# A gate load moved from SP's DMA queue to ScalarE's, ahead of its scores, with four buffers

## The chip, the cores and the metric

The kernel runs on 1 core of one Trainium2 chip. The metric is the device time of one execution in microseconds, as the median over several runs. The core has five engines that take their instructions in order and wait for each other by semaphores: TensorE (PE), VectorE (DVE), ScalarE (ACT), GpSimd (POOL) and SyncE (SP). SP does no arithmetic here: it issues the DMAs, the transfers between HBM and the core's own memory, and each of them lands some time after its issue.

## The reference

The model has two layers over 2048 tokens of width 1024 and a context of 256. Layer 0 mixes with differential attention and a short convolution, layer 1 with a neighbourhood attention and a Fourier mix. The change lies in layer 1's neighbourhood attention, of which this is the core, for one row of the 32 x 64 token grid:

```python
def one_row(args):
    q_r, r0, roff = args
    kb = lax.dynamic_slice_in_dim(kg, r0, kh, axis=1)
    ...
    s_w = s_w + jnp.transpose(bias, (0, 2, 1, 3))[None]
    s_c = jnp.einsum('bqhd,bkhd->bhqk', q_r, k_c) * scale
    p = jax.nn.softmax(jnp.concatenate([s_w, s_c], axis=-1), axis=-1)
    ...
out_x = jnp.concatenate([o_n * jax.nn.silu(gn), fourier_mix(ud) * jax.nn.silu(gd)], axis=-1)
```

There are 8 heads of width 64. `silu(gn)` is the gate: a 512 x 2048 array that layer 1's input projection has written to HBM, and with which the attention's output is multiplied element by element.

## The kernel before

Layer 1's attention (`attention1`) works on 4 head pairs `hp`, and in each on 16 blocks `i` of 128 tokens, so on 64 blocks n = 16 hp + i. A block has two halves `hh`, one for each head. For each half `scores` computes six products on PE into PSUM (L1922), VectorE adds the bias or mask and takes the maximum (L1929), ScalarE takes the Exp with its sum (L1931), VectorE the reciprocal of the sum (L1933), GpSimd scales the row (L1934). `transposes` runs two blocks later: PE transposes the row in two pieces into tiles `pt` of a pool with two buffers (L1956), ScalarE copies the first piece to `pT`, VectorE the second (L1959, L1961). `values` runs three blocks later: PE multiplies `pT` with v into `po` (L1976). Four blocks share one `po`; below they are called a group, j = 0 to 15. At a group's last block VectorE multiplies `po` with the group's gate, in place of the gate (L1982), and SP stores the product to `mixa` in HBM (L1983). The gate g, 128 x 512 numbers or 256 KB, is loaded by SP at the group's first `values` (L1969), into two buffers; a buffer can be loaded again when the store out of it has landed.

While a pair is worked on, the next pair's data are loaded, in `scores` at the pair's first block: `na_q` (four halves of q at L1830, 512 KB each), `na_k` (eight of k at L1844, 576 KB each), `na_rest` (v at L1870, 1152 KB; the masks bm at L1880 and L1881) and the bias rows be of the edge blocks (`na_edge`, L1862, 128 KB each). All these are issued by SP too.

The code calls the steps in the order of the blocks, but the order of each engine's instructions is set by a scheduler with a model of durations (`schedule_with_timeline_sim`). Only what goes through `pin` keeps its order on its engine: here PE's products and transposes. DMAs aren't pinned in this stage. A DMA carries one of eight semaphores in turn (DMAHW0 to DMAHW7), whichever engine issues it, and waits for the DMA eight places before it in the scheduled order.

The stage begins while the Fourier mix ends: its last products Y are multiplied with another gate (`g<-gd`, L1784, L1786) and stored (L1787). It ends with the load of the output projection's weights (ws, L1241), which then runs on PE until 3309 us.

Of the kernel before, what the change touches and what calls it, by code (L numbers as in the profile page):

```python
# [9 lines left out]
F32 = mybir.dt.float32  # L10
# [7 lines left out]
P = 128  # L18
# [136 lines left out]
class Backbone:  # L155
# [45 lines left out]
    def pin(self, i):  # L201

        e = i.ins.engine
        if e in self.pinned:
            self.tc.add_manual_dep(i.ins, self.pinned[e].name, mybir.DependencyInfo(
                mybir.DependencyClass.NoSync, mybir.DependencyReason.DATA), reason="order")
        self.pinned[e] = i.ins
# [1676 lines left out]
    def attention1(self, qa, ka, rs, ws, ps_t):  # L1884

        nc, a = self.nc, self.a
        NK = self.NK
        with ExitStack() as es:
            qb = self.pool(es, "nqb", 1, "left")
            kb = self.pool(es, "nkb", 1, "left")  # L1890
            vp = self.pool(es, "nv", 2, "left")
            mp = self.pool(es, "nm", 2, "left")
            sp = self.pool(es, "ns", 4, "left")
            ep = self.pool(es, "ne", 2, "left")
            ps_s = [self.pool(es, f"nps{h}", 1, space=PSUM) for h in range(2)]
            ps_o = self.pool(es, "npo", 2, space=PSUM)
            self.pinned = {}
            pin = self.pin

            class It:  # L1900
                pass

            its = {}
            anchors = []

            def scores(n, hh):
                if hh == 0:
                    its[n] = It()
                it = its[n]
                hp, i = n // 16, n % 16  # L1910
                it.hp, it.i = hp, i
                st = self.na[hp]
                edge = i in self.EDGES
                nk = 512 if edge else NK
                kt0 = min(max(i - 2, 0), 12)
                if hh == 0:
                    it.s = []
                ps = ps_s[hh].tile([P, 1024], F32, tag="ps", name="ps")
                c0 = 768 - nk
                for p0, p1, kk in ((c0, 512, kt0 * P), (512, 768, kt0 * P + 512 - c0), (768, 1024, S)):  # L1920
                    for part in range(2):
                        pin(nc.tensor.matmul(ps[:, p0:p1], st["q"][hh][:, i * P:i * P + P],  # L1922
                                             st["k"][hh][part][:, kk:kk + p1 - p0], start=part == 0, stop=part == 1))
                w = nk + L
                s = sp.tile([P, NK + L], F32, tag="s", name="s", bufs=6)
                bias = (st["e"][i] if edge else st["m"])[hh]

                mx = ep.tile([P, 1], F32, tag="mx", name="mx", bufs=4)
                nc.vector.tensor_tensor_reduce(s[:, :w], ps[:, c0:1024], bias, -1.0, BIGGEST, ALU.add, ALU.min, mx)  # L1929
                Z = ep.tile([P, 1], F32, tag="Z", name="Z", bufs=6)  # L1930
                nc.scalar.activation(s[:, :w], s[:, :w], AF.Exp, bias=mx, scale=-1.0, accum_out=Z)  # L1931
                rz = ep.tile([P, 1], F32, tag="rz", name="rz", bufs=4)
                anchors[:] = [nc.vector.reciprocal(rz, Z).ins,  # L1933
                              nc.gpsimd.tensor_scalar(s[:, :w], s[:, :w], rz, 1.0, ALU.mult, ALU.mult).ins]  # L1934
                it.s.append(s)

                it.blocks = [(b * P, P, kt0 + b) for b in range(4)] + [(nk, P, 16), (nk + P, P, 17)]
                if not edge:
                    it.blocks.append((512, 64, kt0 + 4))
                if hh == 0:  # L1940
                    it.pT = [None, None]
                    return
                if i == 1 or i == 2:
                    self.na_edge(hp, 13 + i)
                if i == 0 and hp < 3:
                    self.na_q(hp + 1, qb if hp % 2 == 0 else qa)
                    self.na_k(hp + 1, kb if hp % 2 == 0 else ka)
                    self.na_rest(hp + 1, vp, mp)

            def transposes(n, hh):  # L1950
                it = its[n]
                pT = it.pT[hh] = sp.tile([P, 7, P], F32, tag="pT", name="pT")
                for g in (0, 4):
                    pt = ps_t.tile([P, 512], F32, tag="pt", name="pt")
                    for x, (o, m, kt) in enumerate(it.blocks[g:g + 4]):
                        pin(nc.tensor.transpose(pt[0:m, x * P:x * P + P], it.s[hh][:, o:o + m], self.ident))  # L1956
                    full = 4 if g == 0 else 2
                    srcp = pt.rearrange("p (k q) -> p k q", q=P)
                    (nc.scalar.copy if g == 0 else nc.vector.tensor_copy)(pT[:, g:g + full], srcp[:, 0:full])  # L1959
                    if len(it.blocks) > g + full and g:  # L1960
                        nc.vector.tensor_copy(pT[0:64, 6], srcp[0:64, 2])  # L1961

            def values(n):
                it = its[n]
                hp, i = it.hp, it.i
                if i % 4 == 0:
                    it.po = ps_o.tile([P, 512], F32, tag="po", name="po")
                    it.g = ep.tile([P, 512], F32, tag="g", name="g", bufs=2)
                    nc.sync.dma_start(it.g, self.gn[hp * P:hp * P + P, i * P:i * P + 512])  # L1969
                else:  # L1970
                    it.po, it.g = its[n - 1].po, its[n - 1].g
                oc = it.po[:, (i % 4) * P:(i % 4) * P + P]
                nb = len(it.blocks)
                for x, (o, m, kt) in enumerate(it.blocks):
                    for hh in range(2):
                        pin(nc.tensor.matmul(oc[64 * hh:64 * hh + 64], self.na[hp]["v"][0:m, kt, 64 * hh:64 * hh + 64],  # L1976
                                             it.pT[hh][0:m, x, :], start=x == 0, stop=x == nb - 1,
                                             tile_position=(0, 64 * hh)))
                if i % 4 < 3:
                    return  # L1980
                g = it.g
                nc.vector.tensor_tensor(g, it.po, g, ALU.mult)  # L1982
                nc.sync.dma_start(self.mixa[1][i // 4][hp * P:hp * P + P], g)  # L1983
                for k in range(n - 3, n):
                    its.pop(k)

            self.na_rest(0, vp, mp)
            fs, steps = ExitStack(), []
            for n in range(67):
                for hh in range(2):  # L1990
                    if n > 52 and steps:
                        self.pinned.update({i.engine: i for i in anchors})
                        steps.pop(0)()
                        if not steps:
                            fs.close()
                    if n < 64:
                        scores(n, hh)
                    if 2 <= n < 66:
                        transposes(n - 2, hh)
                if n >= 3:  # L2000
                    values(n - 3)
                if n == 49:

                    rs.close()
                    steps = self.load_wout(1, ws, fs)[1]
# [53 lines left out]
```

## Time and profile before

| what | value |
|---|---|
| median of 3 runs | 3306.8 us (3304.11 to 3309.04) |
| the profiled execution's own time | 3310.85 us |
| its span | 3309.1 us |
| PE busy | 3144.4 us, 95% of the span |
| DVE, ACT, POOL busy | 1922.6, 1581.1, 1450.1 us |
| DMA | 442.08 MB, mean 134 GB/s |
| layer 1's attention in the span | about 2757 to 3121 us |

The profile is of one execution, which took 4.05 us more than the median; times in the trace are counted from the span's start. A busy share over the whole span says little about a change in one stage. What has to be read is that stage's own stretch, the waits in it, and the order of SP's issues. In a row of a timeline stand the start and the length in us, the engine, the line, the operation, what it writes and reads, and in brackets the idle time before it and what ended it.

### The profile page before, as it was taken

The numbers are of one execution on the slowest core, as the hardware profiler recorded it, in microseconds if no ns is written. First come the engines' busy times: TensorE is split into PE (matmuls) and PEld (weight loads), VectorE is DVE, ScalarE is ACT, GpSimd is POOL, SyncE is SP. The second block draws the span as 40 slices with busy tenths as digits, with TensorE's granted clock in tenths as the row PEclk, the third lists the DMA queues.
The fourth block names the chain that finished last, engine by engine and source line by source line (L and its number), as shares of the span: only waits on it lengthen the run. The fifth ranks groups of instructions, "written<-read, shape, count | busy, mean of one in ns | idle before, by whom it ended". The sixth has DMA issues, their size and how long they took to land. (4 is left out here: it accounts for less than half of the span.)

```text
span 3309.1 us, 53756 instructions
## 1 busy us (share of the span) xinstructions
PE 3144.4 (95%) x20154; PEld 2618.1 (79%) x20154; DVE 1922.6 (58%) x4315; ACT 1581.1 (48%) x2541; POOL 1450.1 (44%) x1205
## 2 busy tenths in 40 slices
PE   7999999999999999989999799999999998899999
PEld 6988878777788778777877578898888887788787
DVE  4466564588888888888888745321121026566643
ACT  4311143577777778777777543421111124566410
POOL 3234200478887778777877743200121002343300
PEclk9999999999999999999999899999999999999999
DMA  7366653523343343323322144533232248963233
GB/s 259 119 213 224 218 147 115 190 99 107 125 129 109 100 151 100 128 91 112 119 98 69 59 156 153 176 110 125 74 108 98 84 151 228 225 147 105 69 136 121
DMA packets 305318, 442.08 MB, mean 134 GB/s; under 512 B 54837, under 2 KB 212001, under 8 KB 292258
## 3 DMA queue, kind: packets, MB, share of 16 engines
q1 hardware_dynamic: 305058, 438.64, 41.3%
q8 instruction: 160, 2.62, 0.3%
q14 instruction: 100, 0.82, 0.1%
HBM read 307.59 MB, written 131.43 MB: 133 GB/s over the span
## 5 line engine op out<-in xcount | busy, mean ns | idle before, releaser
L421 PE MATMUL mm<-hx,wh 128*128 128x512 f32 (+1 forms) x2784 | 830.6, 382 | 2.0 <-DVE lo L631 2.0
L803 DVE CUSTOM_DVE_ANT_0 s<-ps,zero 128x768 f32<-128x768 f32 x768 | 717.9, 952 | 165.2 <-PE ps L1044 159.8
L1108 POOL TENSOR_TENSOR s<-s 128x992 f32<-128x992 f32 x256 | 595.3, 2340 | 7.2
L421 PEld LDWEIGHTS mm<-hx,wh 128*128 128x128 f32 x2784 | 510.4, 189 | 109.2 <-DVE lo L631 2.5
L421 PE MATMUL mm<-hx,wl 128*128 128x512 f32 (+1 forms) x1392 | 530.7, 381 | 0.0
L1044 PE MATMUL ps<-kst,qst 128*128 128x512 f32 (+1 forms) x1536 | 429.7, 368 | 75.2 <-DVE mx L803 67.1
L1122 ACT ACTIVATE aT<-pt 128x512 f32<-128x512 f32 (+1 forms) x640 | 336.3, 549 | 149.8 <-PE pt L1115 148.6
L1103 POOL TENSOR_SCALAR s<-s,cf 128x992 f32<-128x992 f32 x256 | 300.6, 1185 | 241.5 <-DVE cf L1093 112.3
L734 PE MATMUL cmm<-cx,wh 128*128 128x256 f32 x1728 | 354.5, 291 | 6.1 <-ACT z L753 4.9
L1044 PEld LDWEIGHTS ps<-kst,qst 128*128 128x128 f32 x1536 | 237.1, 193 | 142.5 <-DVE mx L803 89.7
L1115 PE MATMUL pt<-sm,s 128*128 128x128 f32 x2304 | 340.4, 277 | 5.8 <-ACT aT L1122 5.1
L1083 ACT ACTIVATE s<-s,bias 128x2304 f32<-128x2304 f32 x128 | 284.3, 2221 | 53.1 <-DVE bias L1072 52.9
L421 PEld LDWEIGHTS mm<-hx,wl 128*128 128x128 f32 x1392 | 262.7, 189 | 53.9
L1115 PEld LDWEIGHTS pt<-sm,s 128*128 128x128 f32 x2304 | 271.0, 143 | 41.9 <-ACT aT L1122 12.8
L734 PEld LDWEIGHTS cmm<-cx,wh 128*128 128x128 f32 x1728 | 277.4, 193 | 17.5 <-ACT z L753 7.9
L1083 ACT ACTIVATE s<-s,low 128x2304 f32<-128x2304 f32 x128 | 283.5, 2215 | 2.1
L1132 PE MATMUL po<-aT,vt 128*64 128x256 f32 x2304 | 277.4, 385 | 0.8 <-DVE f L827 0.8
L734 PE MATMUL cmm<-cx,wl 128*128 128x256 f32 x864 | 248.7, 288 | 0.0
L1132 PEld LDWEIGHTS po<-aT,vt 128*64 128x64 f32 x2304 | 153.9, 136 | 93.9 <-issue 26.3
L1934 POOL TENSOR_SCALAR s<-s,rz 128x832 f32<-128x832 f32 (+1 forms) x128 | 121.5, 950 | 180.0 <-DVE rz L1933 155.9
L1275 PE MATMUL y<-wh,mh 128*128 128x512 f32 x544 | 182.5, 414 | 1.2 <-DVE mx L803 1.2
L1275 PE MATMUL y<-wh,mx 128*128 128x512 f32 x544 | 174.0, 398 | 0.0
(265 smaller groups left out, 4792.7 us busy)
## 6 DMA issues: line engine op xcount, KB each, us to landing
cx<-hx SPq DMA_DIRECT2D x72, 1024.0 KB
hx<-hx SPq DMA_DIRECT2D x18, 1024.0 KB
kst<-k SPq DMA_DIRECT2D x192, 96.0 KB
k<-k SPq DMA_DIRECT2D x32, 576.0 KB
xt<-in_x_dram SPq DMA_DIRECT2D x32, 512.0 KB
wm<-in_w_mod_dram SPq DMA_DIRECT2D x64, 256.0 KB
qst<-q SPq DMA_DIRECT2D x256, 64.0 KB
ws<-in_w_in_even_dram SPq DMA_DIRECT2D x27, 512.0 KB
```

The lines of the kernel that those rows point to most:

```text
L421: mm = self.nc.tensor.matmul(ps[:, :n], p[:, kc], y, start=first, stop=last)
L734: yield nc.tensor.matmul(ps, w[p][:, kc, :], x[q][:, kc, :], start=i == 0, stop=i == 23)
L803: return self.nc.vector.tensor_tensor_reduce(dst, ps, self.zero.to_broadcast([P, n]), -QS, BIGGEST, ALU.add, ALU.min, mx)
L1044: pin(nc.tensor.matmul(ps[:, k0:k1], q[:, qc:qc + P], k[:, k0:k1], start=True, stop=True))
L1083: pin(nc.scalar.activation(it.s[m], it.s[m], AF.Exp, bias=bias, scale=-1.0, accum_out=it.Z if m else it.rz[:, 0:1]))
L1103: pin(nc.gpsimd.tensor_scalar(x, x, it.cf, 1.0, ALU.mult, ALU.mult))
L1108: pin(nc.gpsimd.tensor_tensor(it.s[0][:, cs], it.s[0][:, cs], it.s[1][:, cs], ALU.add))
L1115: pin(nc.tensor.transpose(pt[:, i * P:i * P + P], it.s[0][:, k0:k0 + P], self.ident))
L1122: pin(nc.scalar.activation(it.aT[g][:, 0:k, n * P:n * P + P], it.pt.pop(g)[:, 0:k * P].rearrange("p (k q) -> p k q", q=P), AF.Copy))
L1132: pin(nc.tensor.matmul(it.po[c:c + 64, 0:256], vts[it.h][:, kt, :], it.aT[g][:, i, :], start=kt < 2, stop=kt >= 16, tile_position=(0, c)))
L1275: self.pin(self.nc.tensor.matmul(ps[hf] if isinstance(ps, list) else ps[:, cs], x, w[kc][:, cs], start=kc == 0 and i == 0, stop=kc == 7 an ...
L1934: nc.gpsimd.tensor_scalar(s[:, :w], s[:, :w], rz, 1.0, ALU.mult, ALU.mult).ins]
```

## The change

The gate of a group is no longer loaded in `values` by SP, but in `scores`, at the group's first block, by ScalarE, and the pool has four buffers for it and not two.

```diff
@@ scores
                 if hh == 0:
                     it.s = []
+                    if i % 4 == 0:
+
+                        it.g = ep.tile([P, 512], F32, tag="g", name="g", bufs=4)
+                        nc.scalar.dma_start(it.g, self.gn[hp * P:hp * P + P, i * P:i * P + 512])
@@ values
                 if i % 4 == 0:
                     it.po = ps_o.tile([P, 512], F32, tag="po", name="po")
-                    it.g = ep.tile([P, 512], F32, tag="g", name="g", bufs=2)
-                    nc.sync.dma_start(it.g, self.gn[hp * P:hp * P + P, i * P:i * P + 512])
                 else:
```

In the changed file the lines behind the load in `scores` stand four further on (the Exp is L1935, the copies of pT are L1963), the product and the store two further on (L1984, L1985); the gate's load is L1921. PE's instructions keep their order.

ScalarE's queue in the change, where the stage begins (pb belongs to the Fourier mix, s is the row of an Exp):

```order
L1766 ACTIVATE pb<-pc 128x512 x2
L1921 DMA g<-gn 128x512 x2
L1935 ACT_TABLE_LOAD
L1935 ACTIVATE s,Z<-s,mx 128x768
L1921 DMA g<-gn 128x512 x2
L1935 ACTIVATE s,Z<-s,mx 128x768 x3
L1963 COPY pT<-pt 128x512 x2
```

The gates of groups 0 to 3 stand before the first and the second Exp, and not with the scores of blocks 0, 4, 8 and 12. The other twelve stand after 15, 26, 32, 44, 47, 55, 64, 76, 79, 87, 95 and 103 Exps of the stage's 128; the first scores of group j belong to Exp 8j.

ScalarE's queue in the change, from the 26th Exp on, at the gate of group 5 (numbers tell the tiles apart; in brackets the semaphores waited for):

```order
L1963 COPY pT_27625<-pt_27626 128x512 [waits PE_49,Activation_49]
L1935 ACTIVATE s_27617,Z_27620<-s_27617,mx_27618 128x832 [waits DVE_49,Pool_49]
L1921 DMA g_28192<-gn_100 128x512 [waits DMAHW4_49,DMAHW3_49]
L1963 COPY pT_27667<-pt_27668 128x512 [waits PE_49,Activation_49]
L1935 ACTIVATE s_27659,Z_27662<-s_27659,mx_27660 128x832 [waits DVE_49,Pool_49]
```

The gate waits for DMAHW3, which is the store of group 1, and for DMAHW4, the second of the k loads of pair 1. Behind it on ScalarE stand the next copy of pT and the next Exp. Before, no DMA stood on this queue.

SP's queue at the end of the burst for pair 2, as the difference from before to the change (mixa_72 is the store of group 3, mixa_69 that of group 4):

```order
 L1844 DMA k<-k_98 64x2304 x2
 L1862 DMA be<-bt 64x512 x8
-L1969 DMA g<-gn 128x512
 L1870 DMA vt<-v_99 128x18x128
-L1983 DMA mixa_72<-g 128x512
-L1969 DMA g<-gn 128x512
-L1983 DMA mixa_69<-g 128x512
-L1969 DMA g<-gn 128x512
-L1983 DMA mixa_70<-g 128x512
-L1969 DMA g<-gn 128x512
+L1985 DMA mixa_72<-g 128x512
+L1985 DMA mixa_69<-g 128x512
```

The gates are gone from SP; the store of group 3 keeps its place behind the whole burst. The same holds for group 7 and pair 3, and the store of group 1 stands behind the eight k loads of pair 1.

## Rows read from the trace of the kernel before

**Rows 1.** Stretches: length, PE/PEld/DVE/ACT/POOL busy (count), clock, DMA share, GB/s.
```profile
2760.00:2780.00 20.00, 13.43 (x88) 11.97 (x88) 13.77 (x35) 10.40 (x20) 9.27 (x23) 0.83 0.97 282
...
2880.00:2897.00 17.00, 2.37 (x21) 2.16 (x19) 2.57 (x6) 1.43 (x2) 0.21 (x1) 0.68 0.94 234
...
2930.00:2975.00 45.00, 45.00 (x484) 40.45 (x481) 29.52 (x86) 28.68 (x56) 21.12 (x30) 1.00 0.91 206
```

**Rows 2.** Timeline around VectorE's first wait for a gate; the first row for comparison.
```profile
2818.30 1.90 PE L1976 MATMUL po<-pT,vt 128*64 128x128 f32 x28
...
2870.34 19.42 SPq L1862 DMA_DIRECT2D be<-bt  x8
...
2889.80 0.59 SPq L1969 DMA_DIRECT2D g<-gn  x1
...
2894.43 0.69 DVE L1982 TENSOR_TENSOR g<-po,g 128x512 f32<-128x512 f32 x1 [15.35 <-DMA g<-gn]
...
2896.74 0.87 PE L1956 MATMUL pt<-sm,s 128*128 128x128 f32 x3 [14.63 <-DVE pT L1961]
...
2897.54 2.91 PE L1976 MATMUL po<-pT,vt 128*64 128x128 f32 x28
```

**Rows 3.** Timeline around VectorE's second wait for a gate.
```profile
2979.25 0.69 DVE L1982 TENSOR_TENSOR g<-po,g 128x512 f32<-128x512 f32 x1 [5.04 <-DMA g<-gn]
...
2981.55 0.86 PE L1956 MATMUL pt<-sm,s 128*128 128x128 f32 x3 [4.32 <-DVE pT L1961]
```

**Rows 4.** SP's issues of group 1's store and the gate behind it; ScalarE in between.
```profile
2829.07 0.53 SPq L1983 DMA_DIRECT2D mixa<-g  x1
...
2829.86 0.19 ACT L1931 ACTIVATION_READ_ACCUMULATOR s<-s,mx 128x1 f32 x1
2831.88 0.59 ACT L1959 COPY pT<-pt 128x512 f32<-128x512 f32 x1 [1.83 <-PE pt L1956]
...
2847.72 0.33 SPq L1969 DMA_DIRECT2D g<-gn  x1
```

**Rows 5.** Stores 6 and 7: chain of waits (first row), SP's timeline (the others).
```profile
2937.35 5.69 DMA mixa<-g
...
2937.35 0.53 SPq L1983 DMA_DIRECT2D mixa<-g  x1
...
2983.58 0.32 SPq L1969 DMA_DIRECT2D g<-gn  x1
```

**Rows 6.** VectorE's timeline: mask wait, last two products of the Fourier mix.
```profile
2774.65 1.02 DVE L1929 CUSTOM_DVE_ANT_0 s<-ps,bm 128x832 f32<-128x832 f32 x1 [0.39 <-DMA bm<-bt]
...
2804.64 1.41 DVE L1786 TENSOR_TENSOR Y<-Y,g 128x512 f32<-128x512 f32 x1 [0.43 <-DMA g<-gd]
...
2807.91 0.69 DVE L1786 TENSOR_TENSOR Y<-Y,g 128x512 f32<-128x512 f32 x1 [0.39 <-DMA g<-gd]
```

**Rows 7.** ScalarE's timeline where the change puts gates 10 and 11.
```profile
2940.32 0.19 ACT L1931 ACTIVATION_READ_ACCUMULATOR s<-s,mx 128x1 f32 x1
2942.42 0.59 ACT L1959 COPY pT<-pt 128x512 f32<-128x512 f32 x1 [1.91 <-PE pt L1956]
...
2968.67 0.19 ACT L1931 ACTIVATION_READ_ACCUMULATOR s<-s,mx 128x1 f32 x1
2970.69 0.59 ACT L1959 COPY pT<-pt 128x512 f32<-128x512 f32 x1 [1.84 <-PE pt L1956]
```

**Rows 8.** SP's timeline: store 5 and the gate behind it, with no burst.
```profile
2916.49 0.32 SPq L1983 DMA_DIRECT2D mixa<-g  x1
2918.83 0.32 SPq L1969 DMA_DIRECT2D g<-gn  x1
```

**Rows 9.** SP's waits in the stage: us in total, times, longest.
```profile
SPq L1969 <- DMA mixa<-g: 30.8, 12, 5.4
```

## The prediction

> **What bounds the kernel now.** The kernel is one long row of stages, and the change touches one of them: layer 1's attention, 2757 to 3121 us. I read the stretches first: in steady running a stage's stretch is nearly all TensorE (2930 to 2975: PE busy 45.0 of 45 us), so whatever stops PE there ends up in the time, and after the stage the output projection follows on PE with nothing that could take up a delay [rows 1]. Then the waits. VectorE waits twice for a gate, 15.35 and 5.04 us, and PE stands idle 14.63 and 4.32 us right behind [rows 2, 3]. The place is the same both times: SP hands out the next head pair's loads (q, k, bias, v) and the gate of the pair's first group stands behind them. The last eight bias issues took SP 19.42 us, then the gate left at 2889.80 and VectorE had it at 2894.43 [rows 2].
>
> Blocks are numbered n = 0 to 63, groups (four blocks, one gate, one store) j = 0 to 15; each block has two Exps. A gate buffer is free again when the store that read it has landed. So the second thing to read is how long stores take: store 1 leaves SP at 2829.07, behind the burst of pair 1, and the gate that waits for it can go only at 2847.72 [rows 4]; store 6 leaves just ahead of pair 3's burst at 2937.35, store 7 behind it, and the gate that waits for store 7 goes at 2983.58, 46.2 us after store 6 left [rows 5]. Today SP sits through these waits, and it has nothing else to do. That is what changes.
>
> **What goes.** Both gate waits of VectorE: the gates of groups 4 and 8 now leave tens of us ahead. On PE that is 14.63 + 4.32 = 18.95 us. After such a gap PE restarts at the lower of its two clock levels, 1.2 and not 2.4 GHz (granted 0.68 over 2880 to 2897): 28 value products took 2.91 us at 2897.54 where 1.90 is usual, 1.0 us lost each time [rows 1, 2], twice 1.0. Together **-21.0**.
>
> Of the 15.35 us, 10.7 (2879.1 to 2889.80) were SP's turn and 4.6 the transfer. The Trainium skill, "DMA: Bandwidth & Descriptors", section "Issuing engines are not separate DMA queues", says that DMAs of all issuers share the same 16 engines and a second issuer saves only the time to issue. By that rule a gate asked for at the same moment would still take its 4.6 and about 4 us, and the sum would be some 8 us worse; here the order moves the load ahead as well, so I count both parts.
>
> **What comes: waits on ScalarE.** The scheduler doesn't leave a load with its group's first scores. It puts it where its own model has the buffer free: gates 0 to 3 before the second Exp, gates 4 to 15 after 15, 26, 32, 44, 47, 55, 64, 76, 79, 87, 95 and 103 Exps, some sixteen Exps ahead of the scores they belong to. Gate j waits for store j-4, and ScalarE executes in order, so behind a waiting gate stand the next copy of pT and the next Exp. PE transposes into two buffers, one of which only ScalarE's copy frees: PE stops within a block. The stores stay on SP, with the burst ahead of them.
>
> *Gate 5* (after 26 Exps) waits for store 1. The 26th Exp ends with its accumulator read at 2829.86 + 0.19 = 2830.05; store 1 has landed at 2847.72 [rows 4]. That is 17.7 us. ScalarE would have idled 1.83 of it anyway, and the issue costs 0.32 (SP's price): 16.2 us late. One thing shortens it: VectorE's last product of the Fourier part, after whose store the burst may leave, moves one place ahead (from 2807.91 to about 2804.64, [rows 6]), 3.3 us, which gives 12.9. I take the middle, **+14.5**.
>
> *Gates 7 and 11* (after 44 and 76 Exps) wait for stores 3 and 7, which stand behind a whole burst. Pair 3's burst shows it undisturbed: from store 6's issue to store 7 landed 46.2 us; from that issue to the end of the 76th Exp 2968.67 + 0.19 - 2937.35 = 31.5 us [rows 5, 7]. The wait is 14.7; less 1.84 idle, plus 0.32: 13.2 each. In the old run pair 2's burst began late, as SP stood at a gate until 2847.72; with ScalarE's stop for gate 5 the blocks are late instead, so pair 2 will look like pair 3. Two of them: **+26.4**.
>
> *Gates 6 and 10* (after 32 and 64 Exps) wait for stores 2 and 6, with one k load ahead. Store 6 landed 5.69 us after 2937.35; ScalarE is free at 2940.51; 2.5 us of wait, 1.91 covered, 0.32 issue: 0.9 each [rows 5, 7], **+1.8**.
>
> *Restarts.* Three long stops at 1.0 us each [rows 2]: **+3.0**.
>
> *Gates 4, 8, 9, 12 to 15*: the load stands after the Exp that follows the group's product, and SP is free. Store 5 left at 2916.49 and the next gate at 2918.83, 2.3 us [rows 8]; ScalarE comes there some 3 us after the product starts. I take 0; the most is about 0.6 each, 4 in all.
>
> *The start of the stage*. Six more transfers of 256 KB (two gates, two weight loads and one pair of the Fourier part) come ahead of the mask that VectorE waited for at 2774.65. At the 282 GB/s of that stretch they are 1.57 MB / 282 = 5.6 us at most [rows 1, 6]; the wait there was 0.39 us, and the same bytes are missing later, so 0 is the least. I take **+2.0**.
>
> The sum is -21.0 + 14.5 + 26.4 + 1.8 + 3.0 + 2.0 = **+26.7 us**. The profiled execution took 3310.85, which gives 3337.6; it lies 4.05 above the median of 3306.8, and for that I forecast **3333.5 us**.
>
> The Trainium skill has a rule that speaks against the change: the same page, section "Two DMAs through the same engine are not ordered", has the issuing engine itself wait for the first DMA's semaphore before it issues the dependent one, so the wait moves with the load. The trace agrees: SP stands 30.8 us in 12 waits for these stores now [rows 9]. If just these moved, less 12 covers of 1.84, they would add 9 us and the sum would be -21 + 9 + 2 = -10; I go by the positions above instead, since the order and four buffers change which store each gate meets. The -10 belongs to the first rival.
>
> **Rivals.**
>
> *The waits don't bite: faster.* If stores 1, 3 and 7 landed before ScalarE comes to gates 5, 7 and 11, only the gains stay: -21.0 + 2.0 = -19, **3288** (3297 with the -10 above). The point from which this decides: store 7 must land 31.5 + 1.84 = 33.3 us after store 6 leaves, not 46.2. The burst carries 9.8 MB (q 2.1, seven k 4.1, twelve be 1.6, v, a gate and two stores 2.0), 211 GB/s today; it needs 293. The fastest stretch here ran at 282, this one at 206 [rows 1]. A load built where the words of the change put it, at its group's first scores, would do it too; the order shows that it isn't. Chance 0.09.
>
> *Half of it.* If pair 1's burst starts early enough that gate 5 waits for nothing, gates 7 and 11 remain: -21.0 + 26.4 + 1.8 + 2.0 + 2.0 = +11, **3318**. Chance 0.08.
>
> *More of it.* All upper bounds: gate 5 16.2, gates 7 and 11 without cover 14.7 each, the start 5.6, the seven other gates 4: -21.0 + 16.2 + 29.4 + 1.8 + 3.0 + 5.6 + 4 = +39, **3346**. Chance 0.11.
>
> *Nothing to measure.* Waits of half the size would just pay for the gain. No row gives such a size. Chance 0.05.
>
> **How the numbers follow.** The forecast has 0.67. Its own range goes from gate 5 at 12.9, 11.9 for gates 7 and 11 (one gate of 256 KB less in SP's queue, 1.3 us at 206 GB/s), 0 for gates 6 and 10 and the start (+18.7, 3325) to gate 5 at 16.2, the start at 5.6 and 2 for the other gates (+34.0, 3341). With half of it and more of it the range is 3317 to 3346. 0.2% is 6.6 us, about what a measurement can tell from no change: slower than 3313.4 are the forecast, half and more, 0.86 with rounding to 0.85; the same 0.06; faster 0.09.
>
> **What will show it.** In the profile after: no wait of VectorE for g<-gn at the product. ScalarE idle before pT copies for DMA mixa<-g: about 15 to 18 us once near 2845, and about 13 to 15 us twice, some 75 us apart; PE idle at its transposes right behind each, for pT of ScalarE. SP no longer waiting for mixa<-g. Wrong would be: three stops of other lengths (the size of a burst misjudged), stops at gates 8, 9 or 12 to 15 (the idle cover misjudged), or none at all, with the stage some 19 us shorter.

## The result, and the profile after

| | median | runs | ratio to before (95% interval) |
|---|---|---|---|
| before | 3307.57 us | 3304.11 to 3309.04 | |
| the change | 3332.36 us | 3328.26 to 3335.66 | 1.0071 (1.0057 to 1.0086) |

The change is slower by 24.8 us; 3333.5 was forecast. The profiled execution took 3334.66 us, its span is 3332.9 us, 23.8 more than that of before.

First the waits of the stage, the view that names what now ends idle time (us in total, times, longest). Before its copies of pT ScalarE waits three times for a store, PE waits for ScalarE's copy, and VectorE's product waits for no gate any more:

```profile
ACT pT L1963 <- DMA mixa<-g: 40.1, 3, 14.4
...
PE pt L1960 <- ACT pT L1963: 36.5, 7, 12.3
...
DVE g L1984 <- PE po L1978: 5.3, 8, 2.0
```

Then ScalarE's timeline at these three places. Each time the last row of an Exp, the gate's issue (ACTq), and the copy that stood behind it:

```profile
2833.88 0.19 ACT L1935 ACTIVATION_READ_ACCUMULATOR s<-s,mx 128x1 f32 x1
2847.78 0.33 ACTq L1921 DMA_DIRECT2D g<-gn  x1
2848.48 0.59 ACT L1963 COPY pT<-pt 128x512 f32<-128x512 f32 x1 [14.41 <-DMA mixa<-g]
...
2892.55 0.19 ACT L1935 ACTIVATION_READ_ACCUMULATOR s<-s,mx 128x1 f32 x1
2905.61 0.33 ACTq L1921 DMA_DIRECT2D g<-gn  x1
2906.03 0.58 ACT L1963 COPY pT<-pt 128x512 f32<-128x512 f32 x1 [13.30 <-DMA mixa<-g]
...
2985.75 0.19 ACT L1935 ACTIVATION_READ_ACCUMULATOR s<-s,mx 128x1 f32 x1
2997.91 0.33 ACTq L1921 DMA_DIRECT2D g<-gn  x1
2998.33 0.58 ACT L1963 COPY pT<-pt 128x512 f32<-128x512 f32 x1 [12.39 <-DMA mixa<-g]
```

They are gates 5, 7 and 11. The chain of the stage (start, length, what) has the stores they wait for. Stores 1, 3 and 7 are issued behind a burst (the loads of the next head pair), at 2828.80, 2899.64 and 2991.58; stores 2 and 6 leave just ahead of one:

```profile
2828.80 18.95 DMA mixa<-g
...
2860.30 5.51 DMA mixa<-g
...
2899.64 5.94 DMA mixa<-g
...
2953.68 5.17 DMA mixa<-g
...
2991.58 6.30 DMA mixa<-g
```

From store 2's issue to store 3 landed it is 2899.64 + 5.94 - 2860.30 = 45.3 us, from store 6's to store 7 landed 44.2 us; undisturbed before it was 46.2 [rows 5].

PE's timeline: a usual row of transposes, then behind each of the three waits its transposes and the value products after them:

```profile
2831.65 0.93 PE L1960 MATMUL pt<-sm,s 128*128 128x128 f32 x7
...
2849.21 1.73 PE L1960 MATMUL pt<-sm,s 128*128 128x128 f32 x7 [12.30 <-ACT pT L1963]
2850.86 3.09 PE L1978 MATMUL po<-pT,vt 128*64 128x128 f32 x28
...
2906.76 1.73 PE L1960 MATMUL pt<-sm,s 128*128 128x128 f32 x7 [11.20 <-ACT pT L1963]
2908.42 3.27 PE L1978 MATMUL po<-pT,vt 128*64 128x128 f32 x28
...
2999.06 1.73 PE L1960 MATMUL pt<-sm,s 128*128 128x128 f32 x7 [10.42 <-ACT pT L1963]
3000.72 3.20 PE L1978 MATMUL po<-pT,vt 128*64 128x128 f32 x28
```

Seven transposes usually take 0.93 us here and 28 products 1.90 [rows 2]. Behind a stop they take 0.80 and 1.2 to 1.4 us more: the granted clock over the 4.7 to 4.8 us there is 0.56, 0.52 and 0.53, about the lower level. PE's transposes start 12.5, 11.4 and 10.6 us later than in a usual block, so each stop costs 14.5, 13.5 and 12.7 us in all. The stretches (columns as in [rows 1]) show the first stop as a granted clock of 0.78, 1.00 in the same stretch of before, and show the start of the stage, which is the other loss:

```profile
2757.00:2785.00 28.00, 16.65 (x110) 15.25 (x108) 16.34 (x38) 12.64 (x24) 10.26 (x21) 0.82 0.95 284
2825.00:2856.00 31.00, 18.70 (x176) 16.66 (x175) 11.23 (x33) 10.14 (x20) 7.17 (x14) 0.78 0.78 182
```

In the 28 us from 2757 PE is busy 16.65 us, and in the 28 us that lie as far behind the last Fourier copy it was busy 21.06 us before (2760.81 to 2788.81), although the transfers run at the same pace, 284 GB/s (281 before).

Where the 23.8 us come from is best read between VectorE's 16 products po times gate, since one ends each group. The two profiled executions reach the stage 3.81 us apart (ScalarE's last copy of the Fourier mix starts at 2755.39 before and at 2751.58 now), so the first step is counted from that copy:

| step | before | after | difference | forecast |
|---|---|---|---|---|
| last Fourier copy to product 0 | 42.56 | 50.58 | +8.0 | +2.0 (start) |
| product 0 to 1 | 22.30 | 22.11 | -0.2 | 0 |
| product 1 to 2 | 20.27 | 34.72 | +14.45 | +15.5 (gate 5, restart) |
| product 2 to 3 | 19.55 | 20.04 | +0.5 | +0.9 (gate 6) |
| product 3 to 5 | 55.70 | 53.08 | -2.6 | -1.4 (gate 4's wait gone, gate 7's new) |
| product 5 to 7 | 39.44 | 40.04 | +0.6 | +0.9 (gate 10) |
| product 7 to 9 | 45.62 | 52.20 | +6.6 | +8.9 (gate 8's wait gone, gate 11's new) |
| product 9 to 15 | 120.35 | 120.64 | +0.3 | 0 |
| sum | 365.79 | 393.41 | +27.6 | +26.8 |

From product 15 to the end of the span both need 187.9 us: nothing is taken up later. The total was close, but the start was forecast 6.0 us too small and the three steps with stops 4.6 too large together.

### The profile page after: what moved, and what is told of

Read it like the earlier page. It is cut to its first block, busy times and chain, and to the rows that moved or that the text cites. A ratio compares the mean times of both kernels' runs of the same rounds, so it can differ in the third digit from the quotient of the medians.

```text
span 3332.9 us, 53762 instructions
## 1 busy us (share of the span) xinstructions
PE 3150.5 (95%) x20154; PEld 2622.9 (79%) x20154; DVE 1922.5 (58%) x4315; ACT 1580.1 (47%) x2541; POOL 1449.2 (43%) x1205
```

## The experiments

**One part alone: four buffers, still SP's queue.** The place of the load in the code was not tried by itself: the scheduler gives the same order of instructions whether the gate is written in `scores` or in `values`, so the change has two parts, the queue and the buffers.

```diff
@@ values, from before
-                    it.g = ep.tile([P, 512], F32, tag="g", name="g", bufs=2)
+                    it.g = ep.tile([P, 512], F32, tag="g", name="g", bufs=4)
```

> One part of the change alone: the gate stays on SP's queue, in the values step as before, but has four buffers. Theory (the loss is ScalarE standing behind gates that wait for stores, the gain is that a gate with four buffers is asked for long before it is needed): no wait of ScalarE for a store, no wait of VectorE for a gate, PE without the 14.63 and 4.32 us stops; SP stands in the waits for stores, as before. 3307 - 21 + 0 to 4 for a later start = 3286 to 3291. Rival (the earlier loads themselves cost the time, by crowding the transfers of the stage's start and of the bursts): 3307 to 3320, with VectorE or PE waiting for q, k, be or bm. Rival (VectorE's gate waits went away because of ScalarE's queue): VectorE still waits some 15 and 5 us for a gate, 3307.

Measured: 3290.62 us, 0.9942 (0.9918 to 0.9965) of before on the same chip (3311.42). PE's waits in the stage, then the issue of gate 4 on SP (2894.43 was when VectorE got it before [rows 2]):

```profile
PE pt L1956 <- DVE pT L1961: 10.9, 12, 3.6
...
PE ps L1922 <- DMA k<-k: 2.6, 1, 2.6
```

```profile
2800.85 0.32 SPq L1969 DMA_DIRECT2D g<-gn  x1
```

The gate now leaves before pair 1's burst, and no gate is waited for. The steps of products 3 to 5 and 7 to 9 become 16.2 and 6.1 us shorter, 22.3 together where 21.0 was forecast. The start is 2.0 us longer, the step from product 2 to 3, in which PE waits 2.6 us for k at pair 1's first scores (0.2 before), is 3.9 us longer, and the stage as a whole is 15.7 us shorter. SP stands 33.5 us for stores (30.8 before [rows 9]), and PE waits for no gate. So four buffers bring the whole gain without ScalarE. Both rivals fall; of the first only the wait for k is seen.

**The other part alone: ScalarE's queue, two buffers.**

```diff
@@ scores, from the change
-                        it.g = ep.tile([P, 512], F32, tag="g", name="g", bufs=4)
+                        it.g = ep.tile([P, 512], F32, tag="g", name="g", bufs=2)
```

> The other part alone: the gate on ScalarE's queue, with two buffers as before. The order puts gates 3, 5 and 9 after the 26th, 44th and 76th Exp, where gates 5, 7 and 11 stand with four buffers, and they wait for the same stores 1, 3 and 7. Theory: the same three waits of ScalarE, 12 to 15 us each, and no wait of VectorE for a gate, as even two buffers are filled some ten Exps ahead of the product; the start is less crowded (two gates there, not four), so 2 to 4 us less than the change: 3326 to 3332. Rival (with two buffers the gates come too late as before): VectorE waits for gates in addition, 3340 to 3350. Rival (four early gates at the start are what costs): no long stop, about 3307 or less.

Measured: 3335.73 us, 1.0076 (1.0051 to 1.0101). ScalarE's waits:

```profile
ACT pT L1963 <- DMA mixa<-g: 42.6, 4, 14.7
...
ACT s L1935 <- DMA mixa<-g: 2.5, 1, 2.5
```

The three long ones are 12.60, 14.69 and 12.54 us, at the same stores, and VectorE waits for no gate. So the queue alone makes the loss. The 2 to 4 us less did not come: product 0 is 6.5 us late (8.0 in the change), but two small waits of 2.73 and 2.50 us are added.

**The load held where its words put it.** An order without a wait ties gate j to the Exp before its group's first scores.

```diff
@@ scores, from the change
-                        nc.scalar.dma_start(it.g, self.gn[hp * P:hp * P + P, i * P:i * P + 512])
+                        g = nc.scalar.dma_start(it.g, self.gn[hp * P:hp * P + P, i * P:i * P + 512])
+                        if exps:
+                            self.tc.add_manual_dep(g.ins, exps[-1].name, mybir.DependencyInfo(
+                                mybir.DependencyClass.NoSync, mybir.DependencyReason.DATA), reason="order")
...
-                nc.scalar.activation(s[:, :w], s[:, :w], AF.Exp, bias=mx, scale=-1.0, accum_out=Z)
+                exps.append(nc.scalar.activation(s[:, :w], s[:, :w], AF.Exp, bias=mx, scale=-1.0, accum_out=Z).ins)
```

> The change with one thing added: each gate's load is held, by an order without a wait, behind the Exp just before its group's first scores (gate j after 8j Exps), so that it stands where the words of the change put it. Theory: stores 1, 3 and 7 have landed by then (14, 12 and 12 Exps later, 30 us and more), so the three waits for stores go; what can remain are waits of a few us where a gate meets the DMA eight places ahead of it, a k or be load of a running burst (gates 3 and 5, and 8 or 9): 0 to 15 us in all. 3287 to 3303. Rival (a load on ScalarE's queue costs by itself, wherever it stands): 3325 to 3335 with ScalarE idle before its copies. Rival (the early loads at the start cost most of it): about 3305, with the three waits still there.

Measured: 3333.62 us, 1.0068 (1.0041 to 1.0095): no better than the change. ScalarE's waits for stores are gone, and three waits for bias loads stand in their place (4.74, 21.71 and 16.52 us, at gates 1, 5 and 9):

```profile
ACT pT L1966 <- DMA be<-bt: 43.0, 3, 21.7
```

The chain shows what gate 5 stood behind:

```profile
2856.37 14.72 DMA q<-q
...
2871.10 13.72 DMA k<-k
...
2884.89 8.73 DMA be<-bt
2893.62 0.15 ACTq L1921
```

Among the DMAs that SP and ScalarE issue, each waits for the one eight places ahead of it in the scheduled order, whichever of the two issues either; those on GpSimd's queue have eight semaphores of their own. Gate 5 stands eight places behind a be load late in pair 2's burst, that be load eight behind a k, and that k eight behind a q. So a gate that is scheduled into a burst has to wait until SP has got through the burst so far, and ScalarE with it. The expectation of 0 to 15 us missed this: it took the eight loads ahead for nearly landed. The first rival's remark that a load at its group's first scores would not bite is wrong.

**The stores away from the bursts.**

```diff
@@ values, from the change
-                nc.sync.dma_start(self.mixa[1][i // 4][hp * P:hp * P + P], g)
+                nc.gpsimd.dma_start(self.mixa[1][i // 4][hp * P:hp * P + P], g)
```

> The change with its stores moved from SP's queue to GpSimd's, so that no store stands behind a burst. The gates stand after the same Exps as in the change. Theory: stores 1, 3 and 7 leave within some us of their product and land before ScalarE comes to gates 5, 7 and 11 (4, 6 and 6 Exps after the store, 10 to 15 us); the three waits shrink to 0 to 4 us each. GpSimd pays about 1 us per issue, which its idle time covers. 3287 to 3303. Rival (the waits are for DMA engines that are full, not for SP's turn): a store issued into a running burst takes as long to land, the three waits stay at 10 us or more, 3320 to 3335.

Measured: 3315.96 us, 1.0017 (1.0000 to 1.0033), between what the theory and the rival expected, against 3311.42 of before on that chip, where runs of both spread more than elsewhere (before 3299.04 to 3322.41); so the trace says more than the time. In it the stage is 4.3 us longer than before, 27.6 in the change. Store 1 in the chain (18.95 us in the change), and ScalarE's waits:

```profile
2819.83 10.81 DMA mixa<-g
```

```profile
ACT pT L1963 <- DMA be<-bt: 16.0, 2, 10.1
```

Gate 5's wait is gone (14.41 in the change). Gate 7 still waits 10.12 us and gate 11 5.91, for be. Product 0 is 8.4 us late, 8.0 in the change. A store's issue takes GpSimd 0.57 to 0.81 us. So the theory held for gate 5 and for a part of the others: behind each wait for store 3 or 7 stood a second one, only 3 and 6 us shorter, of the kind that the held run showed.

**Gates on ScalarE's queue, but outside the bursts.** Gates 0 to 5 on SP as in the first run, the others held behind chosen Exps.

```diff
@@ attention1, from before
+            AT = {6: 55, 7: 57, 8: 59, 9: 60, 10: 85, 11: 89, 12: 97, 13: 104, 14: 111, 15: 118}
...
+                d = (nc.scalar if j in AT else nc.sync).dma_start(
+                    gt[j], self.gn[hp * P:hp * P + P, i * P:i * P + 512])
...
+                while gates and len(exps) >= AT[gates[0]]:
+                    load_gate(gates.pop(0))
```

> Gates 0 to 5 on SP's queue with four buffers, as in the run with four buffers on SP; gates 6 to 15 on ScalarE's queue, each held behind a chosen Exp (55, 57, 59, 60, 85, 89, 97, 104, 111, 118) at which no burst runs: the store that frees the buffer and the DMA eight places ahead have landed by then. Theory (ScalarE loses time only where a gate meets a store not yet landed, or the DMA eight places ahead in a running burst): no wait of ScalarE for a DMA over 2 us, no wait of VectorE for a gate, and the time of the run with four buffers on SP within 4 us, 0.993 to 0.996 of the time before. Rival (each load on ScalarE's queue costs ScalarE, and PE behind it, some us by itself): ten loads at 2 to 4 us, 20 to 40 us more, 1.000 to 1.006.

Measured: 3290.53 us, 0.9940 (0.9925 to 0.9954). Of the ten issues the two that follow each other closest, and ScalarE's longest sum of waits, which is for PE, as ever:

```profile
2913.64 0.34 ACTq L1910 DMA_DIRECT2D g<-gn  x1
2915.12 0.35 ACTq L1910 DMA_DIRECT2D g<-gn  x1
```

```profile
ACT pT L1974 <- PE pt L1971: 113.2, 65, 3.4
```

No wait of ScalarE for a DMA is left. A load on its queue costs 0.35 us, and PE nothing that shows: the stage is as long as with four buffers on SP, within 0.1 us. This also bears on a rule of the Trainium skill ("DMA: Bandwidth & Descriptors", section "Issuing engines are not separate DMA queues"): DMAs of all issuers run on the same engines, and another issuer saves only issue time. The runs agree: 0.9942 with all gates on SP, 0.9940 with ten of them on ScalarE.

**The start apart from the stops.**

```diff
@@ scores, from the change
-                        nc.scalar.dma_start(it.g, self.gn[hp * P:hp * P + P, i * P:i * P + 512])
+                        (nc.sync if n < 16 else nc.scalar).dma_start(it.g, self.gn[hp * P:hp * P + P, i * P:i * P + 512])
```

> The change with the gates of the first head pair (groups 0 to 3) on SP's queue; the order puts the other twelve on ScalarE after the same Exps as in the change, but gate 5 after 28 and not 26. This tells the start of the stage apart from the three stops. Theory: the first product comes some 6 us earlier than in the change, counted from the end of the Fourier products before it (8.0 us later than before in the change, 2.0 with four buffers on SP), as the mask no longer stands behind ScalarE's gates; gates 5, 7 and 11 still wait, gate 5 some 4 to 5 us less, the others 11 to 14 us. 9 to 12 us under the change: 1.003 to 1.005 of the time before. Rival (the start's loss is made up in the stop for gate 5, since store 1 leaves when the burst does): only 0 to 4 us under the change, 1.006 to 1.007.

Measured: 3328.81 us, 1.0050 (1.0033 to 1.0066), the upper end of what was expected. Product 0 comes 1.5 us late and product 1 3.2, where the change has 8.0 and 7.8; the stops stay:

```profile
2852.75 0.93 ACT L1935 ACTIVATE s<-s,mx 128x768 f32<-128x768 f32 x1 [12.60 <-DMA mixa<-g]
...
2900.53 0.59 ACT L1963 COPY pT<-pt 128x512 f32<-128x512 f32 x1 [12.12 <-DMA mixa<-g]
...
2993.76 0.59 ACT L1963 COPY pT<-pt 128x512 f32<-128x512 f32 x1 [13.26 <-DMA mixa<-g]
```

The step with gate 5 costs 12.2 and not 14.45 us, less of a drop than the two Exps later would give. Counted over the stage 5.4 us are saved. That lies between the two expectations: the start is a loss of its own, made up in part behind it.

**Semaphores of their own: gates and stores on GpSimd's queue.**

```diff
@@ scores and values, from the change
-                        nc.scalar.dma_start(it.g, self.gn[hp * P:hp * P + P, i * P:i * P + 512])
+                        nc.gpsimd.dma_start(it.g, self.gn[hp * P:hp * P + P, i * P:i * P + 512])
...
-                nc.sync.dma_start(self.mixa[1][i // 4][hp * P:hp * P + P], g)
+                nc.gpsimd.dma_start(self.mixa[1][i // 4][hp * P:hp * P + P], g)
```

> Four buffers, gates and stores both on GpSimd's queue, whose DMAs have semaphores of their own: a gate has the store of its buffer to wait for and no DMA of a burst. Gates 4 to 15 stand after nearly the same Exps as in the change. Theory (what is left when the stores leave SP, 10.1 and 5.9 us, is the wait for the DMA eight places ahead, not a full set of DMA engines): no wait for be, a store lands in 3 to 11 us, and gates stand 2 to 10 Exps behind it; GpSimd stands for 0 to 5 us at three gates, PE less. 0.993 to 0.997 of the time before. Rival (the DMA engines are full in a burst, so that stores and gates land as late on any queue): GpSimd stands 10 us and more at gates 7 and 11, its scaled rows are late, PE idles; 1.000 to 1.005.

Measured: 3295.39 us, 0.9948 (0.9932 to 0.9965). GpSimd's waits at a gate, and what PE waited for GpSimd:

```profile
POOL g L1921 <- DMA mixa<-g: 22.1, 6, 8.8
```

```profile
PE pt L1960 <- POOL s L1938: 1.1, 2, 0.9
```

No gate waits for be. The stores still take up to some 9 us to land in a burst and GpSimd stands for them, longer than expected, but PE notices 1.1 us of 22.1: the rows that GpSimd scales are transposed two blocks later. The stage is 1.3 us longer than with four buffers on SP. So the place of a wait decides, more than its length: ScalarE's copies of pT have no such slack.

**Four buffers on SP, stores on GpSimd.**

```diff
@@ values, from the first run
-                nc.sync.dma_start(self.mixa[1][i // 4][hp * P:hp * P + P], g)
+                nc.gpsimd.dma_start(self.mixa[1][i // 4][hp * P:hp * P + P], g)
```

> Four buffers with the gates on SP, and the stores moved to GpSimd's queue, so that SP does not stand in front of the rest of a burst until store 1 has landed behind that burst. Theory: the 3.9 us by which pair 2's k comes late with four buffers on SP go (PE waits 2.6 us for k there), the rest stays: 3 to 5 us under the run with four buffers on SP, 0.992 to 0.994 of the time before. Rival (16 issues on GpSimd delay the rows that it scales): no gain or a loss of up to 5 us against that run.

Measured: 3292.71 us, 0.9944 (0.9930 to 0.9959): no gain over the first run (0.9942). PE still waits for k at pair 1's first scores:

```profile
2851.72 0.83 PE L1922 MATMUL ps<-k,q 128*128 128x256 f32 x5 [2.52 <-DMA k<-k]
```

SP's wait for store 1 was not what made k late. That theory falls.

**Three buffers on SP.**

```diff
@@ values, from before
-                    it.g = ep.tile([P, 512], F32, tag="g", name="g", bufs=2)
+                    it.g = ep.tile([P, 512], F32, tag="g", name="g", bufs=3)
```

> The gate on SP's queue in its old place, with three buffers. One gate less than with four buffers goes ahead of pair 1's burst (gate 4 behind it, not before it), so pair 1's k loads should land 256 KB / 225 GB/s = 1.2 us earlier than there. Theory (what a gate needs is to be asked for before the burst that it would stand behind, and three buffers are enough for that, as gate 8 leaves SP some 20 Exps before its product): no wait of VectorE for a gate; PE's wait for k at pair 1's first scores 1 to 2 us and not 2.6; the time of four buffers within 3 us, 0.993 to 0.995 of before. Rival (three are too few: gate 4, behind pair 1's burst and the wait for store 1, comes late): VectorE waits 2 to 10 us for the gate of group 4, 0.995 to 0.998.

Measured: 3290.19 us, 0.9933 (0.9916 to 0.9951). Gate 4's issue, and all of PE's waits for other engines in the stage:

```profile
2854.57 0.33 SPq L1969 DMA_DIRECT2D g<-gn  x1
```

```profile
PE pt L1956 <- DVE pT L1961: 12.7, 12, 3.2
PE ps L1922 <- DVE mx L1929: 6.4, 4, 2.9
PE pt L1956 <- ACT pT L1959: 1.2, 2, 0.6
```

The wait for k is gone altogether, and no gate is late: gate 4 leaves behind pair 1's burst and ahead of pair 2's. That fits k having been late for the gates that went ahead of it, though one profile does not show it beyond doubt: product 0 now comes 4.1 us late and product 1 6.7 (2.0 and 2.7 with four buffers), and the stage as a whole is only 0.3 us shorter. It is the smallest edit of those that beat both kernels; the four that stand at 0.993 to 0.994 (three and four buffers on SP, four with the stores on GpSimd, ten gates placed on ScalarE) can't be told apart.

## Why the prediction came out right, step by step

- **What goes, -21.0.** Right: -22.3 in the run with four buffers on SP. Most of the rest lies right behind the two stops: the three transposes there took 0.87 and 0.86 us [rows 2, 3], 0.52 at 2788.53 where PE had stood only 0.37 us, which the forecast left out, and the products behind the second stop took 3.17 us and not 2.91.
- **Gate 5, +14.5 and a restart of 1.0.** The wait was forecast and came, but its size fits by luck: 14.45 us with everything where 15.5 was forecast, from a wait that was 2.0 too large at PE and a restart 1.0 too small. ScalarE was 14.41 - 1.83 + 0.33 = 12.9 us late, the lower of the two values that were weighed and not their middle. Nor did the wait shrink for the reason given, an earlier start of pair 1's burst. Its first q's in the change and before:

```profile
2808.44 2.39 SPq L1830 DMA_DIRECT2D q<-q  x4
```

```profile
2809.00 2.37 SPq L1830 DMA_DIRECT2D q<-q  x4
```

  From the last Fourier copy that is 56.9 us, 53.6 before, so the burst began 3.3 us later. Store 1 landed 3.8 us later, but the 26th Exp ended 7.8 us later (2834.07 - 2751.58 = 82.5, 74.7 before), as the start had cost that much. The start and this wait were forecast as terms that do not touch; a longer start shortens the wait.
- **Gates 7 and 11, 13.2 each and a restart.** Right in kind, 0.7 and 1.5 us too large: 13.5 and 12.7 with everything. In them the waits were 1.8 and 2.6 too large and the restarts 1.1 too small. From the store ahead of the burst to the store behind it took 45.3 and 44.2 us, not 46.2, and ScalarE came there 32.4 and 32.3 us after the former, not 31.5. The two stops came 92 us apart, not some 75.
- **Why they wait.** Half right. The store landed last, as forecast, and for gate 5 it is the whole cause. For gates 7 and 11 a be load eight places ahead is nearly as late: with the stores moved 10.1 and 5.9 us stay. The prediction read the waits off the store alone.
- **Gates 6 and 10, 0.9 each.** 0.5 and 0.6.
- **Restarts, 1.0 each.** They took 2.0, 2.2 and 2.1 us. The forecast had the 28 products alone, with 1.0 from [rows 2]; here these lost 1.2 to 1.4, and the seven transposes ahead of them 0.80.
- **The start, +2.0, at most 5.6.** This term failed: it cost 8.0 up to product 0. It was worked out as bytes ahead of the mask at the pace of that stretch, and the pace did stay (284 GB/s). What moved was SP's turn. In the change's order the first masks stand behind a store of Y at which SP stands 5.68 us; before, and with four buffers on SP, they stand ahead of that store, and SP stands some 5 us at the first mask itself. In the change, rows of ScalarE, of SP, and of PE's idle time at the mask, then the mask's issue before and with four buffers on SP:

```profile
2755.59 1.28 ACT L1935 ACT_TABLE_LOAD   x1 [3.41 <-DMA g<-gn]
...
2760.80 5.68 SPq L1787 DMA_DIRECT2D mixb<-Y  x1
...
2767.01 0.46 SPq L1880 DMA_DIRECT2D bm<-bt  x1
...
2773.16 1.76 PE L1926 MATMUL ps<-k,q 128*128 128x320 f32 x6 [5.04 <-DVE mx L1933]
```

```profile
2761.78 4.96 SPq L1880 DMA_DIRECT2D bm<-bt  x1
```

```profile
2757.38 5.00 SPq L1880 DMA_DIRECT2D bm<-bt  x1
```

  So the mask is out 15.9 us after the last Fourier copy (2767.01 + 0.46 - 2751.58), 11.4 before and 11.5 with four buffers on SP, and VectorE's first masked row starts 20.5 us after that copy, 15.4 before. Those 5.1 us are the larger part of the 8.0. The table load of ScalarE's first Exp stands behind two gates, but that Exp starts only 0.8 us later than before (6.7 us after the copy, 5.9 before). Where the rest comes from, and which of SP's waits there ends last, was not tried apart.

  Product 0 is late by 8.0, 6.5, 6.5 and 8.4 us wherever its gate is on ScalarE, by 1.2 to 2.5 with the first gates on SP and four buffers, by 4.1 with three, and by 3.5 on GpSimd. A few products on, the queues differ less: in the runs with no long stop before product 3 it is late by 5.3 to 6.6 us with the first gates on SP or GpSimd (with four buffers on SP in part by PE's wait for k), and by 7.4 and 9.5 with all gates on ScalarE (held, and with the stores on GpSimd). So by then the earlier loads come with some 6 us on SP and GpSimd too, about the most that was forecast; why was not tried apart. In the change gate 5's stop lies between, and this can't be read.
- **The sum.** +26.8 forecast, +27.6 measured between the same two points. That closeness is in part luck: the start was 6.0 too low, the three stops with their restarts were put at 43.9 and came to 40.7 (the waits 6.5 too high, the restarts 3.3 too low), gates 6 and 10 were 0.7 too high, and the gain was 1.3 too low.
- **The rivals.** Waits that don't bite, half of it, and more of it did not happen. That the waits would go if the load stood at its group's first scores is refuted by the held run.

## What to carry to other kernels

A load with a wait belongs on an engine that has slack where it waits: waits for stores cost nothing that shows on SP, nearly nothing on GpSimd (1.1 of 22.1 us) and most of their length on ScalarE (PE stood 33.9 of 40.1 us), whose next copy PE needed within a block. When a DMA is moved to a compute engine's queue, list every DMA that it waits for, the one eight places ahead in the scheduled order among them, and ask for each where it stands in its own queue. To have a load earlier, first try one buffer more where it is: three buffers in the old place gave 0.9933 of the time, and the move gave 1.0071.

## What was not expected of the hardware

Store 1, issued on GpSimd's queue while pair 1's burst ran, landed after 10.81 us; on SP's queue, behind the burst's issues, it took 18.95 us from its issue. Why was not settled. And a stop of PE of 10 to 12 us costs 2.0 to 2.2 us more behind it, at a granted clock of 0.52 to 0.56: 0.80 in seven transposes and 1.2 to 1.4 in the 28 products behind them.
